# Sums of weight blocks of the second feed-forward, moved from on-chip adds to adding DMAs in memory that are issued during the first feed-forward

## The chip, the cores and the metric

The kernel runs on one core of a Trainium2 chip. The core has five engines with queues of their own: PE (TensorE, matrix products), DVE (VectorE), ACT (ScalarE), POOL (GpSimd) and SP (SyncE, which here only issues DMAs), and 16 DMA engines that move data between memory and the core's on-chip buffer. The metric is the device time in microseconds. Three timed runs of the kernel before lie between 1104.29 and 1104.48 us, median 1104.42.

## The reference

One transformer layer, all in float32, on 512 latent tokens and 256 context tokens of width 1024, in three steps. Each token stream first gets half a step of a gated feed-forward; then the latent tokens are mixed (attention over latent and context keys beside a gated chunk MLP); then the latent tokens alone get a second half step of feed-forward with other weights.

```python
def swiglu(h, w1, w3, w2):
    return (jax.nn.silu(h @ w1) * (h @ w3)) @ w2      # w1, w3: 1024 x 2816, w2: 2816 x 1024

def ffn_sublayer(h_in, shift, scale, gate, norm_w, w1, w3, w2):
    h = modulate(rms_norm(h_in, norm_w), shift, scale)
    return h_in + 0.5 * gate * swiglu(h, w1, w3, w2)

    x = ffn_sublayer(x, ...ffn1...)          # 512 latent tokens
    ctx = ffn_sublayer(ctx, ...ffn1...)      # 256 context tokens, same weights
    ...                                      # token mixing: x from x and ctx
    x = ffn_sublayer(x, ...ffn2...)          # 512 latent tokens, weights ffn2
    return x, ctx
```

## The kernel before

**Precision.** A float32 operand is split in two: `oph` is a copy rounded to the fp32r type (ACT, a CAST) and `opl` is the rest (DVE, a subtraction). `Stream.operand` and `split` (L141 and L142) do this for a weight operand. `mm3` (L176 to L178) makes each product from three matmuls: high by high, high by low, low by high.

**Units.** The hidden width 2816 of a feed-forward is worked off in 22 units `f` of 128 columns. The first four units of each feed-forward are plain products. For the other 18 (4 to 21) the class `Winograd` uses a fast 2 by 2 block product: the two weight matrices w1 and w3 of a unit are cut over the 1024 rows into four quarters of 128x512 elements that lie side by side in one weight block `wst[...]` of 128x2048 elements (1 MB), and seven products (B11, T1, B21, T2, T3, T4, B22) take the place of eight. Each product is 12 matmuls. A matmul has 384 columns in the first feed-forward (two halves of 768 tokens) and 256 in the second (two halves of 512).

The seven weight operands are quarters or sums of quarters. `prep` loads the block on SP's queue (`Stream.block`, L129) and `wants` hands out the operands in order. The sums are four 128x512 operations for each block, in place in the block's buffer: `s1 = q2 + q3`, `q2 = q0 - q2`, `q0 = s1 - q0` and, behind the split of the old `q1`, `q1 = q1 - q0`. They run on POOL in both feed-forwards, apart from block 4 of the second, whose four sums DVE does at the start of its units (`wino.prep(NPLAIN2, nc.vector)`); block 5 of the second is "held": its POOL sums wait for a small copy (`release`) so that they don't start early.

**Order.** A `Flow` is a queue of split operands ahead of PE: five pairs of buffers (`OPS`), up to four more in the second feed-forward (`MORE`). In both runs of units the order of every engine's instructions is that of the program (`nc.ordered`). Products take a pair, and the pair that is freed is filled with the next operand; so a split's lead over PE can't grow beyond the pairs.

**Between the units.** Runs of units are cut by down projections (the product with w2): in the first feed-forward behind units 6, 10 and 16 (`down_thirds`), where the weights come as 512 KB raw tiles (`raw<-wst`, L137). There, and at two slots of each unit, fillers (`ada_step`) work off the modulation vectors: a 512 KB tile of `w_ada` is loaded into one of three `raw` buffers (`raw<-wada`, L137), and DVE multiplies and reduces it. In the first feed-forward's first units POOL, DVE and SP work in these intervals: first down 135.8 to 181.0 us, units 7 to 10 from 181 to 235, second down to 280, units 11 to 16 to 363.4, third down 363.4 to 416.7, units 17 to 21 to about 480. Token mixing follows; the second feed-forward's seven-product units start at about 797 and the kernel's last matmul ends at 1099.45. `L60` in the profile is the helper that records all engine calls, so names of tiles tell more than lines there: `block` is a weight block or a sum in it, `s` is `s1`, `hh`/`hl` are the first feed-forward's inputs, `mm` and `one` are PSUM banks, `gh`/`gl` a unit's output.

```python
            def block_sums():
                if not self.ready[4]:
                    eng[0].tensor_sub(q[2], q[0], q[2])
                eng[0].tensor_sub(q[0], s1[0], q[0])
            def third():
                a = st.operand(q[1])
                eng[0].tensor_sub(q[1], q[1], q[0])
                return a
```

Of the kernel before, what the change touches and what calls it, by code (L numbers as in the profile page):

```python
# [17 lines left out]
P = 128  # L18
# [3 lines left out]
NF = FF // P  # L22
# [6 lines left out]
CHUNKS1 = [5, 5, 6, 6]  # L29
# [5 lines left out]
NPLAIN1 = 4  # L35
NPLAIN2 = 4
BLOCKS = 2
RAWS = 3
OPS = 5
MORE = 4  # L40
GA, GB = (0, 384), (384, 384)

COL_B, COL_N1, COL_N2, COL_N3 = 0, 72, 80, 88
# [138 lines left out]
def layer_kernel(ctx: ExitStack, tc: tile.TileContext, xT, wfirst, wst, wada, wuq, wkpe, cols, wrope, vnw, rope, out):  # L182
    nc = Core(tc)
    left = lambda: tc.using_default_side("left")
    right = lambda: tc.using_default_side("right")

    const = ctx.enter_context(tc.tile_pool(name="const", bufs=1))
    raws = ctx.enter_context(tc.tile_pool(name="raws", bufs=RAWS))
    opp = ctx.enter_context(tc.tile_pool(name="ops", bufs=1))
    st = Stream(nc, raws, opp, OPS, wst)  # L190
# [361 lines left out]
    r0, v = rstd_tiles(0)  # L552
# [286 lines left out]
    class Winograd:  # L839


        def __init__(self, pool, n, u0, blocks, g_tile, sl_bufs, s1_bufs, third=None, held=None):
            self.third, self.held = third, held
            self.sl_bufs, self.s1_bufs = sl_bufs, s1_bufs
            self.ready = (None,)
            self.pool, self.n, self.u0, self.blocks, self.g_tile = pool, n, u0, blocks, g_tile

        def tmp(self, name, n, bufs=1):
            return self.pool.tile([P, n], F32, tag=name, bufs=bufs, name=f"{name}_{nc.next_id()}")

        def prep(self, f, eng=None, early=False):
            r = st.block(wst, (self.u0 + 2 * f) // 2, self.third if f % 3 == 0 else None)
# [6 lines left out]
            self.ready = f, q, s1, nc.gpsimd if early else eng or nc.gpsimd, early  # L859

        def wants(self, f):
            q, s1, eng = [], [], []
# [28 lines left out]
            of = lambda i: lambda: st.operand(q[i])  # L891
            return first, lambda: st.operand(s1[0]), third, of(0), of(2), of(3), of(1)

        def plan(self, flow, f0, downs, late=False):

            self.flow, self.late = flow, f0 if late else -1
            w = self.wants(f0)
            flow.todo.append(w[0])
            for f in range(f0, NF):
                nxt = self.wants(f + 1) if f + 1 < NF else None  # L900
                nx = nxt[:1] if nxt else ()
                if f == self.late:
                    flow.todo.extend((w[3], w[4], w[2]) + nx + (w[1],) + w[5:])
                elif nxt is None:
                    flow.todo.extend((w[3], w[4], w[2], w[1]) + w[5:])
                else:
                    flow.todo.extend(w[1:5] + nx + w[5:])
# [30 lines left out]
        def unit(self, f, hd, step):  # L938
# [7 lines left out]
            def ev_sl():  # L946
                nc.scalar.activation(sl, X, AF.Silu)
                yield

            def ev_u2():  # L950
                v.tensor_add(u2, Y, p1)
                yield

            def ev_u2z():
                v.tensor_add(u2, Y, p1)
                yield
                v.tensor_add(Z, Z, u2)

            def ev_u3():
                nc.scalar.copy(u3, W)  # L960
                v.tensor_add(u3, Z, u3)
                yield

            def ev_lo():
                v.tensor_add(W, W, u2)
                v.tensor_mul(W, W, sl)
                yield
                g_split(W, gh[:, :n], gl[:, :n])
# [11 lines left out]
                yield  # L980

            def ev_u3b():
                v.tensor_add(u3, Z, u3)
                yield

            nxt = None
# [7 lines left out]
            else:  # L994
# [4 lines left out]
            seeded = f != self.late and f + 1 < NF  # L999
# [23 lines left out]
    def ada_step(n=1):  # L1023
        for _ in range(n):
            next(ada, None)
# [15 lines left out]
    t1ctx = ExitStack()  # L1041
    with right():
# [955 lines left out]
    i = LAST  # L1998
# [421 lines left out]
```

## Time and profile before

| what | value |
|---|---|
| median of three runs | 1104.42 us (1104.29 to 1104.48) |
| profiled execution | 1104.5 us |
| its span (first to last instruction) | 1102.5 us, so 2.0 us lie outside |
| TensorE clock granted | 1.00 |
| busiest engine | PE, 1097.5 us of the span |
| DVE, ACT, POOL busy | 892.8, 536.5, 310.3 us |
| DMA traffic on SP's queue | 124.63 MB, 33.2% of what 16 engines' span holds |

Busy times are of one core. A group's row has the count behind an x, then the busy time of all, the mean of one in ns, and behind the second bar the idle time just before such instructions with what ended it. A window's row has the stretch, its length, and for each engine the busy time and the count; then the granted clock, the share of time in which the 16 DMA engines were busy, and GB/s. A row of the timeline or the chain begins with the start and the length in microseconds. A bracket at a row's end is an idle time before it and its releaser.

### The profile page before, as it was taken

What the parts mean: (1) busy time and instruction counts of PE and PEld (TensorE: products, weight loads), DVE (VectorE), ACT (ScalarE), POOL (GpSimd) and SP (SyncE); (2) the same over time, 40 slices, a digit from 0 to 9 for tenths busy, and PEclk for the clock granted to TensorE, in tenths of its full rate; (3) what the DMA queues carried; (4) which work ended last, traced back from release to release, by engine and by line L of the source; (5) the groups of instructions that cost most, each with busy time, mean ns of one, the idle gap of its engine ahead of it and who ended that gap; (6) DMA issues with size and microseconds to landing.
All of it is one profiled execution on the core that took longest, in us unless ns stands there. A gap on an engine that the chain in (4) does not pass through costs nothing.

```text
span 1102.5 us, 19621 instructions
## 1 busy us (share of the span) xinstructions
PE 1097.5 (100%) x7610; PEld 1052.5 (95%) x7610; DVE 892.8 (81%) x1594; ACT 536.5 (49%) x1115; POOL 310.3 (28%) x269
## 2 busy tenths in 40 slices
PE   9999999999999999999999999999999999999998
PEld 7899999999999999999998889999999989898997
DVE  5779998888878769866867899989988878787883
ACT  6545422431344214443765549986663535354450
POOL 0003303311344013400009317860014444352420
PEclk9999999999999999999999999999999999999999
DMA  9721354234334664412241310103222322424202
GB/s 354 279 60 47 120 172 139 100 137 148 106 124 151 233 201 164 149 54 93 97 132 61 102 50 21 39 21 102 91 94 89 123 78 93 137 78 132 99 21 77
DMA packets 35677, 125.95 MB, mean 114 GB/s; under 512 B 3712, under 2 KB 10624, under 8 KB 30976
## 3 DMA queue, kind: packets, MB, share of 16 engines
q1 hardware_dynamic: 35440, 124.63, 33.2%
q8 instruction: 60, 0.98, 0.4%
q14 instruction: 33, 0.27, 0.1%
q10 hardware_dynamic: 144, 0.06, 0.1%
HBM read 122.58 MB, written 2.10 MB: 113 GB/s over the span
## 4 chain that ended last, share of the span: by engine, by line
PE 96%; DMA 1%; DVE 1%; ACT 1%; POOL 0%; issue 0%; SPq 0%; ACTq 0%; POOLq 0%; DVEq 0%
PE mm L60 61%; PE one L60 20%; PE big L60 10%; PE big L616 1%; PE mm L601 1%; DMA scale<-wada 1%; PE mm L177 1%; PE mm L176 1%; PE mm L178 1%; PE mm L338 1%; DMA x<-xT 0%; PE big L608 0%; DVE sq L60 0%; POOL pe L60 0%; ACT hh L60 0%
## 5 line engine op out<-in xcount | busy, mean ns | idle before, releaser
L60 DVE TENSOR_TENSOR opl<-block,oph 128x512 fp32r<-128x512 f32 x216 | 195.4, 912 | 32.6 <-ACT oph L60 29.9
L60 POOL TENSOR_TENSOR block<-block 128x512 f32<-128x512 f32 x69 | 105.0, 1522 | 378.9 <-DVE opl L60 376.2
L60 ACT CAST oph<-block 128x512 fp32r<-128x512 f32 x216 | 132.3, 622 | 108.8 <-PE mm L60 85.5
L60 PE MATMUL mm<-gl,oph 128*128 128x256 f32 (+2 forms) x573 | 176.4, 308 | 0.0
L60 PE MATMUL mm<-gh,opl 128*128 128x256 f32 (+2 forms) x573 | 176.4, 308 | 0.0
L60 PE MATMUL mm<-gh,oph 128*128 128x256 f32 (+2 forms) x573 | 176.4, 308 | 0.0
L60 PEld LDWEIGHTS mm<-gh,oph 128*128 128x128 f32 x573 | 107.6, 188 | 5.5
L60 PEld LDWEIGHTS mm<-gh,opl 128*128 128x128 f32 x573 | 107.6, 188 | 5.4
L60 PEld LDWEIGHTS mm<-gl,oph 128*128 128x128 f32 x573 | 107.6, 188 | 5.4
L60 ACT CAST oph<-raw 128x512 fp32r<-128x512 f32 x127 | 76.0, 620 | 69.7 <-PE mm L60 44.4
L60 DVE SCALAR_TENSOR_TENSOR x<-mm,g,x 128x512 f32<-128x512 f32 (+2 forms) x136 | 78.7, 600 | 28.5 <-PE mm L60 27.9
L60 DVE TENSOR_TENSOR opl<-raw,oph 128x512 fp32r<-128x512 f32 x127 | 88.1, 710 | 15.3 <-ACT oph L60 14.0
L60 POOL TENSOR_TENSOR block<-s,block 128x512 f32<-128x512 f32 x35 | 48.3, 1379 | 123.8 <-DVE opl L60 122.3
L60 PE MATMUL mm<-hh,oph 128*128 128x384 f32 (+2 forms) x195 | 64.9, 333 | 0.0
L60 PE MATMUL mm<-hl,oph 128*128 128x384 f32 (+2 forms) x195 | 64.8, 333 | 0.0
L60 PE MATMUL mm<-hh,opl 128*128 128x384 f32 (+2 forms) x195 | 64.8, 333 | 0.0
L60 DVE SCALAR_TENSOR_TENSOR junk<-raw,cb 128x1024 bf16<-128x1024 f32 x48 | 62.1, 1308 | 0.2 <-DMA raw<-wada 0.2
L60 POOL TENSOR_TENSOR s<-block 128x512 f32<-128x512 f32 x34 | 53.7, 1579 | 11.4 <-DMA block<-wst 11.4
L60 DVE SCALAR_TENSOR_TENSOR raw<-raw,cb 128x1024 f32<-128x1024 f32 x32 | 42.1, 1322 | 8.3 <-DMA raw<-wada 8.2
L60 PE MATMUL one<-hl,oph 128*128 128x384 f32 x144 | 48.1, 334 | 0.0
L60 PE MATMUL one<-hh,oph 128*128 128x384 f32 x144 | 48.1, 334 | 0.0
L60 PE MATMUL one<-hh,opl 128*128 128x384 f32 x144 | 48.1, 334 | 0.0
(699 smaller groups left out, 3361.9 us busy)
## 6 DMA issues: line engine op xcount, KB each, us to landing
raw<-wst SPq DMA_DIRECT2D x77, 512.0 KB, 3.8
block<-wst SPq DMA_DIRECT2D x36, 1024.0 KB, 4.9
raw<-wada SPq DMA_DIRECT2D x56, 512.0 KB, 4.3
scale<-wada SPq DMA_DIRECT2D x16, 512.0 KB, 9.0
x<-xT SPq DMA_DIRECT2D x5, 512.0 KB, 6.4
raw<-wfirst SPq DMA_DIRECT2D x8, 256.0 KB, 8.8
out<-x SPq DMA_DIRECT2D x7, 256.0 KB, 2.3
raw<-wuq SPq DMA_DIRECT2D x2, 384.0 KB, 5.1
```

The source lines that it names most:

```text
L60: return lambda *a, **k: self.tc.keep_in_program_order(f(*a, **k))
L176: nc.tensor.matmul(out, lh, rh, start=first, stop=False, skip_group_check=more)
L177: nc.tensor.matmul(out, lh, rl, start=False, stop=False, skip_group_check=more)
L178: nc.tensor.matmul(out, ll, rh, start=False, stop=last, skip_group_check=more)
L338: pin(nc.tensor.matmul(pa[q, :P], scw[:, kt, 2 - 2 * w : 34 - 2 * w], units[d][w][:, kt * P : kt * P + P], start=w == 0 and kt < 4, stop=w ...
L601: pin(nc.tensor.matmul(o, l[:, c], r, start=k == 0 and m == 0 and w == 0, stop=k == NK - 1 and m == 2, skip_group_check=True))
L616: pin(nc.tensor.matmul(two(pbs[i]), ops[k][lo][:, i * P : i * P + P], lat(r, k), start=False, stop=k == NK - 1 and m == 2, skip_group_chec ...
```

## The change

The 18 blocks of the second feed-forward no longer get their sums on chip. 18 tiles `sums4` to `sums21` of 128x2048 elements (1 MB each) in device memory take them, and POOL's queue issues 144 DMAs from memory to memory of 128x512 elements (256 KB, in rows of 2 KB) during the first feed-forward: for each block four that copy and four that add to what lies there (`accum_op=ALU.add`), in batches of six blocks, step by step. With only additions the four sums come out as q2, q2+q3 and the like with other signs than before, so some on-chip signs are turned: `hA2`, the additions to `u2`, `Z` and `u3` in the evictions, and `u3`'s copy becomes an activation with scale -1. The number of DVE and ACT instructions in the evictions is the same.

The DMAs' places: two behind each of three slots in units 5 to 20 (six a unit, `ada_up`), and two behind each of the eight `ada_step(2)` of a down projection (16 a down, `after1`): 96 and 48.

In the second feed-forward `prep_sums` loads, for each block, 512 KB and 256 KB of the raw block (three quarters) and 1 MB of sums, 1.75 MB where it was 1 MB, all on SP's queue; there are two buffers for the sums, and a third block buffer goes. With that 69 POOL instructions (17 blocks by four, and the copy of `release`) and the four DVE sums of block 4 are gone. PE's instructions are the same 7050 in the same order.

```diff
+    block_sums = [dram.tile([P, 2048], F32, name=f"sums{f}") for f in range(NPLAIN2, NF)]
+        def prep_sums(self, f):
+            a = st.raw_pool.tile([P, 2048], F32, tag="block", bufs=BLOCKS, name=f"block_{nc.next_id()}")
+            src = wst[self.u0 // 2 + f]
+            nc.sync.dma_start(a[:, 0:1024], src[:, 0:1024])
+            i = f - NPLAIN2
+            pool = st.more[0] if i % 2 else self.pool
+            t = pool.tile([P, 2048], F32, tag=f"sums{i % 2}", bufs=1, name=f"s_{nc.next_id()}")
+            nc.sync.dma_start(t, block_sums[i])
+            nc.sync.dma_start(a[:, 1536:2048], src[:, 1536:2048])
+            q = [t_[:, j * 512 : j * 512 + 512] for t_, j in ((a, 0), (t, 0), (a, 1), (t, 1), (t, 2), (a, 3), (t, 3))]
...
             def ev_u3():
-                nc.scalar.copy(u3, W)
-                v.tensor_add(u3, Z, u3)
+                if neg:
+                    nc.scalar.activation(u3, W, AF.Copy, scale=-1.0)
+                    v.tensor_sub(u3, u3, Z)
...
     def after1(flow, f):
         for ci in ends1(f):
-            down_thirds(flow, starts1[ci], CHUNKS1[ci], lambda dt: ada_step(2))
+            down_thirds(flow, starts1[ci], CHUNKS1[ci], lambda dt: (ada_step(2), next(summing, None), next(summing, None)))
+
+    def sum_steps():
+        q = lambda t, i: t[:, i * 512 : i * 512 + 512]
+        for b in range(0, NF - NPLAIN2, BATCH):
+            for dst, src, add in ((2, 0, 0), (0, -2, 0), (2, -2, 1), (0, -3, 1), (1, 2, 0), (1, -3, 1), (3, 1, 0), (3, -1, 1)):
+                for i in range(b, b + BATCH):
+                    t = block_sums[i]
+                    a = q(wst[U_UP2 // 2 + NPLAIN2 + i], -src) if src < 0 or (dst, add) == (2, 0) else q(t, src)
+                    nc.gpsimd.dma_start(q(t, dst), a, accum_op=ALU.add if add else ALU.bypass)
+                    yield
+
+    summing = sum_steps()
...
     def ada_up(f, i):
...
+        if f > NPLAIN1:
+            next(summing, None)
+            next(summing, None)
...
-            nc.vector.tensor_sub(hA2, hA2, hB2)
+            nc.vector.tensor_sub(hA2, hB2, hA2)
...
-    wino = Winograd(f2, 256, U_UP2, blocks, g2_tile, 2, 2, f2, NPLAIN2 + 1)
-    wino.prep(NPLAIN2, nc.vector)
+    wino = Winograd(f2, 256, U_UP2, blocks, g2_tile, 2, 2, True)
+    wino.prep_sums(NPLAIN2)
```

What this does to the order of instructions is seen at three places.

First, POOL's queue in a unit of the first feed-forward (unit 8 into unit 9, about 205 to 222 us in the profile before). `s1` and `block` are the on-chip sums of the first feed-forward's own blocks, which stay; before, they stand in a row:

```order
L60 TENSOR_TENSOR block_2340_2341<-block_2340_2341 128x512
L60 TENSOR_TENSOR s1_2517_2518<-block_2514_2515 128x512
L60 TENSOR_TENSOR block_2514_2515<-block_2514_2515 128x512
L60 TENSOR_TENSOR block_2514_2515<-s1_2517_2518,block_2514_2515 128x512
L60 TENSOR_TENSOR block_2514_2515<-block_2514_2515 128x512
```

and now:

```order
L61 TENSOR_TENSOR block_2389_2390<-block_2389_2390 128x512
L61 DMA sums6_63<-wst 128x512
L61 DMA sums7_64<-wst 128x512
L61 TENSOR_TENSOR s1_2572_2573<-block_2569_2570 128x512
L61 TENSOR_TENSOR block_2569_2570<-block_2569_2570 128x512
L61 TENSOR_TENSOR block_2569_2570<-s1_2572_2573,block_2569_2570 128x512
L61 DMA sums8_65<-wst 128x512
L61 DMA sums9_66<-wst 128x512
L61 DMA sums4_61<-sums4_61 128x512
L61 DMA sums5_62<-sums5_62 128x512
L61 TENSOR_TENSOR block_2569_2570<-block_2569_2570 128x512
```

Two issues now stand ahead of `s1`, and four between the third sum of a block and its last one (`q1`).

Second, POOL's queue at the third down projection (behind unit 16, 363.4 to 416.7 us). Before, the fourth sum of unit 17's block follows the third at once in the queue:

```order
L60 TENSOR_TENSOR block_4322_4323<-block_4322_4323 128x512
L60 TENSOR_TENSOR s1_4502_4503<-block_4499_4500 128x512
L60 TENSOR_TENSOR block_4499_4500<-block_4499_4500 128x512
L60 TENSOR_TENSOR block_4499_4500<-s1_4502_4503,block_4499_4500 128x512
L60 TENSOR_TENSOR block_4499_4500<-block_4499_4500 128x512
```

Now 18 issues stand between those two, of which these are the last ten, with the sum behind them:

```order
L61 DMA sums20_77<-wst 128x512
L61 DMA sums21_78<-wst 128x512
L61 DMA sums16_73<-wst 128x512
L61 DMA sums17_74<-wst 128x512
L61 DMA sums18_75<-wst 128x512
L61 DMA sums19_76<-wst 128x512
L61 DMA sums20_77<-wst 128x512
L61 DMA sums21_78<-wst 128x512
L61 DMA sums16_73<-wst 128x512
L61 DMA sums17_74<-wst 128x512
L61 TENSOR_TENSOR block_4618_4619<-block_4618_4619 128x512
```

The 18 go over one step of the list to the next: ten copies and eight adds. The first down projection has 18 issues between the same two sums as well (six copies, twelve adds), the second 16 (twelve and four).

Third, the start of the second feed-forward's units on DVE, at about 797 us. `ds` is a small difference ahead of it, `sl` a product of a plain unit behind it; before:

```order
L60 TENSOR_TENSOR ds<-s_87 128x4
L60 TENSOR_TENSOR s_10347_10348<-block_10345 128x512
L60 TENSOR_TENSOR opl_10353<-block_10345,oph_10351 128x512
L60 TENSOR_TENSOR block_10345<-block_10345 128x512
L60 TENSOR_TENSOR block_10345<-s_10347_10348,block_10345 128x512
L60 TENSOR_TENSOR sl_10359<-big_9759,sl_10359 128x256
```

and now:

```order
L61 TENSOR_TENSOR ds<-s_108 128x4
L61 TENSOR_TENSOR opl_10519<-block_10510,oph_10517 128x512
L61 TENSOR_TENSOR sl_10523<-big_9924,sl_10523 128x256
L61 SCALAR_TENSOR_TENSOR t3l<-hfB,ds,t3h 128x256
L61 TENSOR_TENSOR t4l<-hfA,t4h 128x256
```

Three of block 4's sums are gone here, and the fourth a few rows below. On SP's queue each block's one load becomes three; before:

```order
L137 DMA raw_11485_11486<-wst 128x1024
L129 DMA block_11114_11115<-wst 128x2048
L129 DMA block_11297_11298<-wst 128x2048
L129 DMA block_11619_11620<-wst 128x2048
L129 DMA block_11791_11792<-wst 128x2048
```

and now (`s` is the tile of sums):

```order
L138 DMA raw_11638_11639<-wst 128x1024
L858 DMA block_11090_11091<-wst 128x1024
L863 DMA block_11090_11091<-wst 128x512
L862 DMA s_11093_11094<-sums7_64 128x2048
L858 DMA block_11270_11271<-wst 128x1024
L863 DMA block_11270_11271<-wst 128x512
L862 DMA s_11273_11274<-sums8_65 128x2048
```

The loads of block 4 and its sums stand ahead of these, in the place of the loads of before.

More of the change, by code (lines that the diff above doesn't have):

```diff
@@ L839, in layer_kernel, with __init__ @@
     class Winograd:
-        def __init__(self, pool, n, u0, blocks, g_tile, sl_bufs, s1_bufs, third=None, held=None):
-            self.third, self.held = third, held
+        def __init__(self, pool, n, u0, blocks, g_tile, sl_bufs, s1_bufs, summed=False):
+            self.third, self.held, self.summed, self.q = None, None, summed, {}
             self.sl_bufs, self.s1_bufs = sl_bufs, s1_bufs
@@ L849, in tmp, with wants_sums, first @@
             return self.pool.tile([P, n], F32, tag=name, bufs=bufs, name=f"{name}_{nc.next_id()}")
+        def prep_sums(self, f):
[8 more added lines that the diff above has]
+            q = [t_[:, j * 512 : j * 512 + 512] for t_, j in ((a, 0), (t, 0), (a, 1), (t, 1), (t, 2), (a, 3), (t, 3))]
+            self.ready = f, q
+        def wants_sums(self, f):
+            def first():
+                if self.ready[0] != f:
+                    self.prep_sums(f)
+                self.q[f] = self.ready[1]
+                return st.operand(self.q[f][0])
+            return [first] + [(lambda i=i: st.operand(self.q[f][i])) for i in range(1, 7)]
         def prep(self, f, eng=None, early=False):
@@ L948, in ev_sl, with add_u2, seed @@
                 yield
+            neg = self.summed
+            def add_u2():
+                if neg:
+                    v.tensor_sub(u2, p1, Y)
+                else:
+                    v.tensor_add(u2, Y, p1)
+            def seed():
+                if neg:
+                    v.tensor_sub(Z, u2, Z)
+                else:
+                    v.tensor_add(Z, Z, u2)
             def ev_u2():
-                v.tensor_add(u2, Y, p1)
+                add_u2()
                 yield
             def ev_u2z():
-                v.tensor_add(u2, Y, p1)
+                add_u2()
                 yield
-                v.tensor_add(Z, Z, u2)
+                seed()
             def ev_u3():
-                nc.scalar.copy(u3, W)
-                v.tensor_add(u3, Z, u3)
+                if neg:
+                    nc.scalar.activation(u3, W, AF.Copy, scale=-1.0)
+                    v.tensor_sub(u3, u3, Z)
+                else:
+                    nc.scalar.copy(u3, W)
+                    v.tensor_add(u3, Z, u3)
                 yield
             def ev_lo():
-                v.tensor_add(W, W, u2)
+                if neg:
+                    v.scalar_tensor_tensor(W, W, -1.0, u2, ALU.mult, ALU.subtract)
+                else:
+                    v.tensor_add(W, W, u2)
                 v.tensor_mul(W, W, sl)
@@ L982, in ev_u3b @@
             def ev_u3b():
-                v.tensor_add(u3, Z, u3)
+                if neg:
+                    v.tensor_sub(u3, Z, u3)
+                    seed()
+                else:
+                    v.tensor_add(u3, Z, u3)
                 yield
@@ L998, in unit @@
                 self.product(banks[3], "T3", True, ev_u3())
-            seeded = f != self.late and f + 1 < NF
+            seeded = neg or f != self.late and f + 1 < NF
             if f + 1 < NF and nxt is None:
```

14 lines of the change are left out of this document (10 added, 4 removed).

## The prediction, made before the changed kernel ran

> **What bounds the kernel now.** I read the page first: engines, chain by engine, the DMA queue, and the groups that the change touches.
>
> ```profile
> span 1102.5 us, 19621 instructions
> PE 1097.5 (100%) x7610; PEld 1052.5 (95%) x7610; DVE 892.8 (81%) x1594; ACT 536.5 (49%) x1115; POOL 310.3 (28%) x269
> q1 hardware_dynamic: 35440, 124.63, 33.2%
> PE 96%; DMA 1%; DVE 1%; ACT 1%; POOL 0%; issue 0%; SPq 0%; ACTq 0%; POOLq 0%; DVEq 0%
> L60 DVE TENSOR_TENSOR opl<-block,oph 128x512 fp32r<-128x512 f32 x216 | 195.4, 912 | 32.6 <-ACT oph L60 29.9
> L60 DVE TENSOR_TENSOR opl<-raw,oph 128x512 fp32r<-128x512 f32 x127 | 88.1, 710 | 15.3 <-ACT oph L60 14.0
> L60 POOL TENSOR_TENSOR block<-block 128x512 f32<-128x512 f32 x69 | 105.0, 1522 | 378.9 <-DVE opl L60 376.2
> ```
>
> PE is busy in 1097.5 of 1102.5 us, and 96% of the chain that ended last is PE. POOL, which the change relieves, holds 0% of the chain. Then I read the windows and, in the chain in order of time, the steps of the second feed-forward.
>
> ```profile
> core 0: us, PE busy (x) PEld busy (x) DVE busy (x) ACT busy (x) POOL busy (x), PEclk, DMA share, GB/s
> 135.00:490.00 355.00, 355.00 (x2454) 355.00 (x2453) 292.32 (x492) 123.14 (x232) 86.07 (x57) 1.00 0.44 149
> 135.80:181.00 45.20, 45.20 (x389) 45.20 (x389) 41.81 (x78) 9.21 (x17) 6.02 (x3) 1.00 0.50 160
> 235.00:280.00 45.00, 45.00 (x388) 45.00 (x387) 38.85 (x65) 9.18 (x16) 6.02 (x3) 1.00 0.44 151
> 363.40:416.70 53.30, 53.30 (x460) 53.30 (x460) 38.45 (x62) 10.28 (x19) 6.02 (x3) 1.00 0.62 213
> 876.00:936.00 60.00, 60.00 (x438) 56.36 (x437) 49.39 (x75) 27.90 (x61) 23.58 (x16) 1.00 0.30 102
> 218.39 2.08 PE mm L60 x12
> 796.91 17.68 PE mm L60 x156
> 814.59 1.36 PE one L60 x12
> 1099.32 0.13 PE mm L178
> ```
>
> The chain from 796.91 to 1099.45 (1099.32 + 0.13) is PE behind PE, and in every window PE's busy time is the window's length. A product of 12 matmuls lasts 2.08 us in the first feed-forward and 1.36 in the second, so a unit of seven takes 14.56 and 9.52 us. So work taken from POOL and DVE can't shorten the second feed-forward while PE is fed; the question is whether the first, which gets 144 DMAs, stays as full.
>
> **Part 1: the second feed-forward, value 0.** 68 POOL sums of 1.4 to 1.6 us go, none of them on the chain. Four DVE sums go from its start:
>
> ```profile
> 797.93 0.69 DVE L60 TENSOR_TENSOR s<-block 128x512 f32<-128x512 f32 x1
> 798.53 0.69 DVE L60 TENSOR_TENSOR opl<-block,oph 128x512 fp32r<-128x512 f32 x1
> 799.13 0.68 DVE L60 TENSOR_TENSOR block<-block 128x512 f32<-128x512 f32 x1
> 799.85 0.69 DVE L60 TENSOR_TENSOR block<-s,block 128x512 f32<-128x512 f32 x1
> 806.68 0.69 DVE L60 TENSOR_TENSOR block<-block 128x512 f32<-128x512 f32 x1
> 993.67 0.69 DVE L60 TENSOR_TENSOR opl<-block,oph 128x512 fp32r<-128x512 f32 x1
> 997.10 0.28 PE L60 MATMUL mm<-b22h,opl 128*128 128x256 f32 x1
> block<-wst SPq DMA_DIRECT2D x36, 1024.0 KB, 4.9
> ```
>
> Together 2.75 us; PE is inside one step of 17.68 us at that time, so they are cover and not chain: 0. The turned signs keep the count of instructions, so 0 as well. The loads grow from 1 to 1.75 MB a unit. The queue's row gives the engines' rate: 124.63 MB in 0.332 x 1102.5 = 366 us is 340 GB/s, so 1.75 MB (1.84e6 bytes) is 5.4 us of a 9.52 us unit. A whole block landed 4.9 us after its issue, and each operand needs its own piece only. The smallest lead that I found of a split over PE is 997.10 - 994.36 = 2.7 us. POOL's sums (four in a row, 6 us) no longer stand between load and split, which is more than the 2.3 us (5.4 less 3.1 for 1 MB) by which the load grows. I take 0; the bound upward would be one late load at the start, 5.4 - 2.7 = 2.7 us.
>
> **Part 2: POOL issues 144 DMAs.** No row shows POOL issuing such a DMA. From below, SP issues one in 0.33 us; from above, POOL's own operation of the same 128x512 size took 1.52. I take 1.5, for it is the same engine that would have to prepare 128 rows. The first feed-forward's own sums stand behind them in POOL's queue:
>
> ```profile
> 201.46 0.33 SPq L129 DMA_DIRECT2D block<-wst  x1
> 202.97 0.68 DVE L60 TENSOR_TENSOR opl<-s,oph 128x512 fp32r<-128x512 f32 x1
> 210.26 0.33 PE L60 MATMUL one<-hh,opl 128*128 128x384 f32 x1
> 205.74 1.29 POOL L60 TENSOR_TENSOR block<-block 128x512 f32<-128x512 f32 x1 [7.17 <-DVE opl L60]
> 207.79 1.32 POOL L60 TENSOR_TENSOR s<-block 128x512 f32<-128x512 f32 x1 [0.77 <-DMA block<-wst]
> 209.19 1.74 POOL L60 TENSOR_TENSOR block<-block 128x512 f32<-128x512 f32 x1
> 211.63 1.30 POOL L60 TENSOR_TENSOR block<-s,block 128x512 f32<-128x512 f32 x1 [0.69 <-DVE opl L60]
> 220.30 1.29 POOL L60 TENSOR_TENSOR block<-block 128x512 f32<-128x512 f32 x1 [7.37 <-DVE opl L60]
> 410.02 2.14 POOL L60 TENSOR_TENSOR block<-block 128x512 f32<-128x512 f32 x1 [53.87 <-DVE opl L60]
> ```
>
> POOL's work per unit is 1.29 + 1.32 + 1.74 + 1.30 = 5.65 us, in 14.56. Six issues add 9.0: 14.65, just full. Four of them fall in the idle 7.37 us ahead of the last sum (6.0), two ahead of `s`, which starts 3.0 us behind 207.03 instead of at 207.79, so 2.2 late. The split of `s` ends at 203.65 and PE reads it at 210.26, a lead of 6.6 us, which covers this. Value 0, and POOL becomes the bound above (14.56 - 5.65)/6 = 1.49 us an issue once the lead is used up. In the third down projection 18 issues (27 us) lie in an idle 53.87 us.
>
> The gap between 912 ns for `opl<-block` and 710 ns for `opl<-raw` (195.4 us in 216) shows DVE and POOL in each other's way: 0.2 x 216 = 44 us. The Trainium skill, "SBUF — State Buffer", section "SBUF: two separate sides", lets the two engines share a port pair under an exclusive lock, taken by a DVE operation with two on-chip inputs only against a POOL operation that reads the on-chip buffer; by that a DMA issue, which reads none, would cost these splits nothing, while the gap that the sums cause would vanish from the second feed-forward. No run here shows yet what an issue does to the splits.
>
> **Part 3: the DMA engines.** 256 KB at 340 GB/s is 0.77 us of all 16 engines; no row shows a transfer from memory to memory. A copy that reads and writes at once costs 0.77, one that pays for both 1.54; an add reads two and writes one, so 1.54 to 2.31. I take the lower ends, for reading and writing are one pass in the loads of the row too. 72 x 0.77 + 72 x 1.54 = 166 us (277 by the upper ends) go into the 355 us of the second row, where loads take 0.44 x 355 = 156 us: 322 of 355, it fits. By the upper ends it is 433.
>
> In places it is tighter. The third down projection has the fullest engines, 0.62 x 53.3 = 33 us, and ten copies and eight adds are 20.0: 53.0 of 53.3. The first has 22.6 + 23.1 = 45.7 of 45.2 us, but DVE's waits there (the first row, from the waits of 135 to 185 us) are small; in the third (the second row, 363 to 425 us) they are not:
>
> ```profile
> DVE junk L60 <- DMA raw<-wada: 0.2, 1, 0.2
> DVE raw L60 <- DMA raw<-wada: 8.2, 6, 2.3
> 419.74 1.88 DVE L60 TENSOR_TENSOR opl<-block,oph 128x512 fp32r<-128x512 f32 x3
> 423.15 0.33 PE L60 MATMUL one<-u3h,opl 128*128 128x384 f32 x1
> ```
>
> Six waits make 8.2 us. DVE's other idle time in that stage is 53.3 - 38.45 - 8.2 = 6.65 us. The splits behind them lead PE by 2.7 us (the first of the three ends at about 420.4). If one of the new transfers stands ahead of each awaited load, DVE loses 6 x 0.77 to 6 x 1.54 = 4.6 to 9.2 us, which 6.65 + 2.7 = 9.35 holds. I take 0. The sums themselves are needed only at 797 and their last issue stands in unit 20, before 475 us (416.7 + 4 x 14.56), so they can't be late.
>
> **The sum:** 0 + 0 + 0 against the profiled 1104.5 us (its span of 1102.5 and 2.0 outside), which lies 0.1 above the median; I put 1104.6, for a small loss is nearer than a gain.
>
> **Rivals.**
> A, the third down's loads come late. It is slower by one mechanism: transfers of POOL's queue stand ahead of the `raw<-wada` loads, and DVE, which does these in order, hands its next splits over late. With two ahead of each (mean 1.11 us over ten copies and eight adds) 13.3 us are lost, 13.3 - 9.35 = +4.0; with two adds 18.5, +9.1; by the upper ends (mean 1.88) 22.6, +13.2. It decides from 9.35 us on: 1108.5 to 1117.7. For it speaks the 0.62, against it the three raw buffers. The Trainium skill, "DMA: Bandwidth & Descriptors", section "Issuing engines are not separate DMA queues", says that DMAs issued by GpSimd and Sync end up on the same 16 engines and interleave there; that would be this rival's mechanism, and no run here shows it yet.
> B, POOL becomes the bound. If an issue must also wait for the end of a DVE split (0.68 us), it takes 1.5 + 0.68 = 2.2 us, and a unit asks for 5.65 + 13.2 = 18.85, 4.3 over. Units with issues come in runs of 4, 6 and 4 between the downs: 17.2 + 25.8 + 17.2 less the lead of 6.6 each time is +40: 1145; at 2.0 us (3.1 over) it is +23.6: 1128. For it: issues have no row here, and 1.49 is close to the 1.5 taken. Against it: POOL's own arithmetic at 1.5 reads and writes 256 KB, an issue none. The Trainium skill's page on SBUF warns in the same section that a DVE operation in a two-port mode keeps GpSimd from writing its DMA descriptors until it ends, which would be such a wait. The Trainium skill, "DMA: Bandwidth & Descriptors", section "Latency and other measured facts", has about 1 us to the first byte for a DMA of GpSimd; by that estimate POOL would be at 5.65 + 6 = 11.65 of 14.56, and nothing of B would be left.
> C, the DMA engines are the bound: 433 us of work in 355 by the upper ends is +78, less little: 1180. Against it, both ends would have to be the worst.
> D, faster: PE waits at the second feed-forward's start for DVE in some way the chain hides; at most the 2.75 us of the four sums: 1101.8. Against it, PE's step there has no gap.
>
> **How the numbers follow.** No change 0.57, A 0.24, B 0.10, C 0.06, D 0.03. Within 0.2% (2.2 us, about what a measurement of this kernel can tell) lies the first; A, B and C are slower, 0.40; D is faster. No change and A hold 0.81, so the range is from 1103.4 (a little of D's gain) to 1118 (A by the upper ends). No change alone would be 1103.4 to 1106.6.
>
> **What would show it.** Right: PE's busy time equal to the window's in all of 135 to 490 us; the waits for `raw<-wada` in 363 to 425 at 8 to 17 us and no PE idle behind them; POOL's issues near 1.5 us; DMA share near 0.9 in the downs; in the second feed-forward `opl` splits near 700 ns and PE unchanged. Wrong: PE idle behind `opl` at 420 (A), POOL without idle time in units 7 to 16 and splits waiting for `s` (B), DMA share at 1.0 with all loads late (C), or a second feed-forward shorter than 302 us (D).

## The result, and the profile after

The changed kernel takes 1348.93 us (median of four runs, 1346.68 to 1353.66), the kernel before 1104.36 in the same session: a ratio of 1.222, 95% interval 1.2183 to 1.2258. The prediction was no change, with a range up to 1118 us. The page of the changed kernel (new beside the lines shown of before: `q0`, the queue of POOL's DMAs, and POOL's issues as a group):

```profile
span 1348.8 us, 19756 instructions
PE 1129.8 (84%) x7610; PEld 1078.7 (80%) x7610; DVE 854.4 (63%) x1590; ACT 536.7 (40%) x1115; POOL 302.3 (22%) x344
q1 hardware_dynamic: 40624, 138.79, 30.5%
q0 software_dynamic: 16128, 37.76, 18.7%
PE 52%; issue 32%; POOL 13%; DMA 2%; DVE 1%; ACT 1%; POOLq 0%; SPq 0%; DVEq 0%; ACTq 0%
L61 POOL DMA_DIRECT2D sums<-wst x108 | 79.2, 737 | 406.2 <-issue 398.4 <-DVE x L61 7.5
sums<-wst POOLq DMA_DIRECT2D x108, 256.0 KB, 6.4
```

PE's share of the chain falls from 96 to 52%, and 32% is "issue", time in which an engine waits for nothing that the profile shows. The group's row says whose: POOL stood idle for 406.2 us ahead of its issues from `wst`, all but 8 of it "issue", and its own time for an issue is short (737 ns). Of the 246.3 us that the span grew (1348.8 - 1102.5), 214.0 are idle time of PE (219.0 against 5.0) and 32.3 longer busy time, at a lower granted clock. The waits (total us, times, longest), then windows: two stretches of the first feed-forward and the second one's units:

```profile
POOL sums L61 <- issue: 419.7, 94, 9.7
ACT oph L61 <- POOL block L61: 159.5, 22, 25.3
ACT oph L61 <- POOL s L61: 109.1, 10, 21.6
PE one L61 <- ACT u L61: 132.6, 7, 42.8
181.00:235.00 54.00, 29.11 (x159) 28.47 (x157) 19.99 (x33) 9.69 (x18) 16.52 (x19) 0.78 0.57 115
350.00:400.00 50.00, 7.60 (x35) 7.61 (x36) 9.11 (x15) 5.23 (x10) 13.66 (x14) 0.59 0.47 85
1042.50:1345.00 302.50, 302.39 (x2162) 282.57 (x2161) 206.10 (x382) 135.08 (x290) 0.00 (x0) 1.00 0.42 141
```

The cause reads down the first four rows: POOL waits ahead of an issue, the sums `block` and `s` behind it in POOL's queue come late, so do ACT's splits of them, and what stands behind these in ACT's queue, and PE. In 350 to 400 us PE works in 7.60 of 50. No engine is full there, and the DMA engines are at 0.47. The second feed-forward is as full as before: 302.39 of 302.50. One such wait in order of time, ACT's queue and then PE's:

```profile
391.35 0.62 ACT L61 CAST oph<-s 128x512 fp32r<-128x512 f32 x1 [21.57 <-POOL s L61]
391.87 0.47 ACT L61 COPY u<-one 128x384 f32<-128x384 f32 x1
392.40 0.69 PE L61 MATMUL one<-u4h,oph 128*128 128x384 f32 x1 [42.78 <-ACT u L61]
392.88 0.52 PE L61 MATMUL one<-u4l,oph 128*128 128x384 f32 x1
393.20 0.52 PE L61 MATMUL one<-u4h,opl 128*128 128x384 f32 x1
```

ACT waited 21.57 us for the sum `s` and did the eviction `u` behind it only then; PE, idle for 42.78 us, waited for that eviction. Its first matmuls after the idle time follow each other by 0.32 us and not 0.173 (2.08 us for 12, before): the granted clock was 0.50 from 392.4 to 395.8 us, and 0.59 over the stretch of 350 to 400. That is where the longer busy time comes from.

POOL's queue in order of time, at the first down projection, shows the wait itself. The first group's issues are copies, from 144.49 on they add:

```profile
129.76 1.56 POOL L61 DMA_DIRECT2D sums<-wst  x3
135.98 1.70 POOL L61 DMA_DIRECT2D sums<-wst  x3 [4.67 <-issue]
144.49 0.89 POOL L61 DMA_DIRECT2D sums<-wst  x1 [6.81 <-issue]
149.35 0.85 POOL L61 DMA_DIRECT2D sums<-wst  x1 [3.97 <-issue]
157.28 0.82 POOL L61 DMA_DIRECT2D sums<-wst  x1 [7.07 <-issue]
```

Three copies go out in 1.6 us, and then POOL stops. The trace has the landing of each transfer: 62 of the 144 issues began 0.28 to 0.34 us after the landing of the very one before (all 62 are adds behind adds, one add under way at a time; those at 149.35 and 157.28 are such), and 105 that long after the landing of one of the last four. Of the copies, three were under way at most. An add landed 6.39 us after its issue on average, a copy 5.37, and from the first issue to the last landing it takes 630 us, from 116 to 746.

To see where time goes, the start of the same matmul, counted from the program's first, is compared in both traces (each has 7610 matmuls in the same order; the 7050 given with the change is not what the traces have); the table gives by how many us it is later than before, at places that are named by the time before.

| kernel | 135.8 | 181 | 235 | 280 | 363 | 416.7 | 450 | 500 | 797 | 1095 |
|---|---|---|---|---|---|---|---|---|---|---|
| changed | -0.1 | 1.8 | 56.3 | 59.0 | 147.2 | 175.0 | 203.1 | 245.6 | 245.5 | 245.5 |
| e1_no_sums | 0.0 | 0.0 | -0.1 | -0.1 | -0.1 | -0.1 | -0.1 | -0.1 | -0.1 | -0.1 |
| e2_ring768 | 0.0 | 7.2 | 15.2 | 20.1 | 30.5 | 47.9 | 47.9 | 58.8 | 58.5 | 58.4 |
| e10_ring1280 | 0.5 | 8.5 | 14.4 | 26.8 | 41.8 | 56.3 | 60.9 | 70.0 | 69.6 | 69.6 |
| e4_copies | 0.2 | 1.6 | 2.9 | 7.7 | 11.7 | 22.6 | 24.6 | 28.0 | 27.7 | 27.7 |
| e14_copies1280 | 0.0 | 8.3 | 8.3 | 17.7 | 22.5 | 33.3 | 35.4 | 40.2 | 39.9 | 39.8 |
| e13_sp_pinned | 0.2 | 0.2 | 0.1 | 0.1 | 0.1 | 0.1 | 6.9 | 7.0 | 6.6 | 6.6 |
| e11_tiny512 | -0.1 | -0.2 | 0.4 | 0.4 | 13.0 | 15.0 | 29.2 | 32.4 | 32.1 | 32.0 |
| e12_tiny1280 | -0.1 | -0.1 | -0.2 | -0.2 | -0.2 | -0.2 | 0.7 | 0.8 | 0.6 | 0.5 |

In the changed kernel the whole loss is made between 135.8 and 490 us by the times of before, in the units and downs that hold the issues; ahead of them and behind them nothing is lost.

### The profile page after: what moved, and what is told of

Same layout as the page of the kernel before. It is cut to its first block, busy times and chain, and to the rows that moved or that the text cites. A ratio compares the mean times of both kernels' runs of the same rounds, so it can differ in the third digit from the quotient of the medians.

```text
span 1348.8 us, 19756 instructions
## 1 busy us (share of the span) xinstructions
PE 1129.8 (84%) x7610; PEld 1078.7 (80%) x7610; DVE 854.4 (63%) x1590; ACT 536.7 (40%) x1115; POOL 302.3 (22%) x344
## 3 DMA queue, kind: packets, MB, share of 16 engines
q1 hardware_dynamic: 40624, 138.79, 30.5%
q0 software_dynamic: 16128, 37.76, 18.7%
## 4 chain that ended last, share of the span: by engine, by line
PE 52%; issue 32%; POOL 13%; DMA 2%; DVE 1%; ACT 1%; POOLq 0%; SPq 0%; DVEq 0%; ACTq 0%
PE mm L61 32%; PE big L61 8%; PE one L61 7%; POOL sums L61 7%; POOL block L61 5%; POOL s L61 1%; PE big L620 1%; PE mm L605 1%; DMA scale<-wada 1%; PE mm L179 1%; PE mm L178 1%; PE mm L177 1%; DMA block<-wst 1%; PE mm L342 0%; DMA x<-xT 0%
## 5 line engine op out<-in xcount | busy, mean ns | idle before, releaser
L61 DVE TENSOR_TENSOR opl<-block,oph 128x512 fp32r<-128x512 f32 x162 | 119.7, 747 | 168.7 <-ACT oph L61 166.9
L61 ACT CAST oph<-block 128x512 fp32r<-128x512 f32 x162 | 99.8, 620 | 263.3 <-POOL block L61 159.5
L61 PE MATMUL mm<-gh,oph 128*128 128x256 f32 (+2 forms) x573 | 179.2, 313 | 8.2 <-DVE x L61 7.6
L61 POOL DMA_DIRECT2D sums<-wst x108 | 79.2, 737 | 406.2 <-issue 398.4
L61 PE MATMUL one<-u4h,oph 128*128 128x384 f32 x36 | 18.2, 506 | 142.8 <-ACT u L61 132.6
L61 DVE TENSOR_TENSOR opl<-s,oph 128x512 fp32r<-128x512 f32 x90 | 67.8, 758 | 107.1 <-ACT oph L61 105.4
L61 PEld LDWEIGHTS one<-u4h,oph 128*128 128x128 f32 x36 | 10.3, 286 | 145.3 <-ACT u L61 134.9
L61 ACT CAST oph<-s 128x512 fp32r<-128x512 f32 x90 | 55.7, 620 | 151.4 <-POOL s L61 109.1
L61 PE MATMUL mm<-u4h,oph 128*128 128x384 f32 x36 | 15.8, 439 | 61.2 <-ACT u L61 61.2
L61 PEld LDWEIGHTS mm<-u4h,oph 128*128 128x128 f32 x36 | 8.9, 246 | 62.8 <-ACT u L61 62.8
```

The source lines that it names most:

```text
L61: return lambda *a, **k: self.tc.keep_in_program_order(f(*a, **k))
```

## The experiments

The theories have letters of their own, which are not those of the prediction's rivals. R: the room in which POOL's DMAs keep their descriptors, the notes that tell the DMA engines what to move (`dynamic_dma_scratch_size`, 512 in the changed kernel), holds three copies or one add, and a further issue waits until one lands. S: adds to memory go one at a time whatever the room. E: the DMA engines need this long for such transfers, whatever the room. D, which came up with e3: the transfers fill the DMA engines and hold up the first feed-forward's loads. The times of e2, e4, e8, e10 and e11 are single runs; each loss below is told from that session's own time before (1104.1 to 1104.3).

**e1_no_sums**, the second feed-forward alone:

```diff
-            nc.sync.dma_start(t, block_sums[i])
+            nc.sync.dma_start(t, src)
...
-                    nc.gpsimd.dma_start(q(t, dst), a, accum_op=ALU.add if add else ALU.bypass)
+                    pass
```

> The 144 adding and copying DMAs are left out; the second feed-forward loads its sums' tile from the raw block, so its values aren't the reference's, but it moves the same bytes. All theories that put the loss into the first feed-forward's DMAs expect the time of before, 1102.2 to 1106.6 us, and a second feed-forward of 302.5 us from its first seven-product unit to the last matmul. If the larger loads (1.75 MB a unit) or the turned signs cost something, it shows here alone: 1107 to 1115.

1104.26 us, a ratio of 1.0001 (0.9991 to 1.001). The second feed-forward with 1.75 MB of loads a unit, without 69 POOL and four DVE instructions, and with turned signs costs nothing and gains nothing. Part 1 of the prediction holds.

**e2_ring768** and **e3_ring1600**, more room:

```diff
-    const.tile([P, 64], F32, name="pad_scratch")
-    nc = bacc.Bacc(..., dynamic_dma_scratch_size=512)
+    nc = bacc.Bacc(..., dynamic_dma_scratch_size=768)
```

The tile `pad_scratch` of 256 bytes goes. e3 has 1600, and three buffers for `s1` in place of four make the room; so it is in e8, e10, e12 and e14.

> Only the space for POOL's DMA descriptors changes, 768 bytes of a partition for 512 (the pad of 256 gives it). Theory R (the space is full: at 512 bytes three copies or one add are under way, and the next issue waits for a landing): five copies and two adds should be under way, an add's interval falls from about 6.9 us to 3 to 3.5, a unit with six adds asks POOL for about 24 us in place of 47, and the time falls to 1150 to 1200 us. Theory S (adds to memory go one at a time whatever the space): adds stay at one, 1320 to 1350. Theory E (the DMA engines themselves need this long for transfers from memory to memory): 1340 to 1360.

> The space for descriptors is 1600 bytes; it comes from the pad and from one of four buffers for s1. R: eleven copies or five adds fit, POOL's wait for space is nearly gone, a unit asks for 5.65 + 6 x 0.8 = 10.5 of 14.56 us, and the time is 1104 to 1125 us. S: adds still one at a time, 1300 to 1350. E: 1330 to 1360.

e2 took 1163.9 us: 256 bytes of room took back 185 of the 244.6 us lost. In its trace five copies were under way at most and two adds, and from one add to the next issue it was 3.99 us (6.20 in the changed kernel). S and E fall. e3 took 1185.25 us (ratio 1.0705 to 1.0765), slower than e2 though POOL's waits for room were nearly gone:

```profile
POOL sums L61 <- issue: 192.3, 74, 9.3
POOL sums L61 <- issue: 25.5, 17, 5.5
PE 69%; DMA 17%; DVE 9%; issue 2%; ACT 2%; POOL 0%; ACTq 0%; SPq 0%; DVEq 0%; POOLq 0%
ACT oph L61 <- DMA block<-wst: 57.0, 13, 9.4
POOL s L61 <- DMA block<-wst: 53.0, 12, 8.2
```

The first row is e2's, the other four are e3's. With more room the waits for "issue" fall from 192.3 to 25.5 us, and waits for the loads of weight blocks, 110.0 us, stand in their place. R expected 1104 to 1125 of e3, and missed: there is a second cost behind the first. Part of e3's loss (about 9 us) also came in the second feed-forward; see e10.

**e4_copies**, every DMA a copy (no sums are formed):

```diff
-                    nc.gpsimd.dma_start(q(t, dst), a, accum_op=ALU.add if add else ALU.bypass)
+                    nc.gpsimd.dma_start(q(t, dst), a)
```

> All 144 are plain copies, none adds, so the sums' values aren't the reference's; space of 512 bytes. R: three under way at all times, about 1.9 us an issue, a unit asks for 5.65 + 11.4 = 17, some 2.5 over: 1110 to 1140 us. S: no adds, so no serial ones: 1104 to 1120 if copies can go freely, but then more than three must be seen under way. E with engines that need 5 us for each transfer: above 1300.

1133.2 us, within what R gave, with three under way at most and 133.8 us of waits. It prices the transfers too. `q0` had 12.2% of 16 engines over 1131.0 us here, and 18.2% over 1161.7 us in e2, for the same bytes:

```profile
q0 software_dynamic: 11520, 37.76, 12.2%
q0 software_dynamic: 16128, 37.76, 18.2%
```

So a copy of 256 KB takes 0.96 us of all engines (138 us over 144), and an add 1.97 ((211 - 69) us over 72). The time of packets isn't a fixed price, though: the same 144 DMAs took 195 us in e3 (16.5% of 1182.0) and 252 in the changed kernel (18.7% of 1348.8).

**e5_contig**, the same sums in fewer rows (a second copy of the blocks with each quarter in one piece):

```diff
-        q = lambda t, i: t[:, i * 512 : i * 512 + 512]
+        q = lambda t, i: t[32 * i : 32 * i + 32, :]
...
+    wq = np.ascontiguousarray(wst[44 + NPLAIN2 : 44 + NF].reshape(18, P, 4, 512).transpose(0, 2, 1, 3)).reshape(18, P, 2048)
```

> The same 144 sums with the space of 512 bytes, but from a copy of the weights in which each quarter lies in one piece, so that a DMA of 256 KB is 32 rows of 8 KB in place of 128 of 2 KB. R (space is counted in rows): about ten copies and six adds fit, the waits of one add at a time are gone. What then is left is a second theory, D, on why 1600 bytes gave 1185 and not 1104: the DMA engines' time. If an add's 1.97 us of all engines (18.2% of 16 engines over 1161.7 us, less 72 copies at 0.96) goes with bytes, D stays: 1150 to 1190 us. If it goes with rows, the engines are freed as well: 1104 to 1125. S (adds always one at a time): above 1300.

1154.31 us (ratio 1.0437 to 1.0468). With a room of 512 bytes as in the changed kernel but a quarter of the rows, up to eight copies or six adds were under way and POOL's waits for "issue" were 17.2 us. In e11 below, with all the rows and a thirty-second of the bytes, it was three copies or one add again. So the room is counted in rows, not in the bytes that are moved. Loads stay late (DMA 14% of the chain, weight blocks landed after 9.2 us), as D has it, and 49 us are lost by 500 us, with four buffers for `s1`.

```profile
q0 software_dynamic: 6912, 37.76, 13.4%
```

The same bytes took 154 us of the engines here (13.4% of 1151.7) and 211 in e2, so an add's 1.97 us holds for rows of 2 KB only.

**e6_half** and **e7_half768**, one DMA at each place, 76 in all (blocks from the seventh on get no sums), with 512 and 768 bytes:

```diff
-            next(summing, None)
-            next(summing, None)
+            next(summing, None)
...
-... lambda dt: (ada_step(2), next(summing, None), next(summing, None)))
+... lambda dt: (ada_step(2), next(summing, None)))
```

> One DMA at each place in place of two, 76 in all; blocks from the seventh on load raw weights for their sums, so values aren't the reference's. Space of 512 bytes. R: three adds of 5 to 6.9 us, one behind the other, are 15 to 21 us of a unit's 14.56, but copies come between and POOL waits only where the space is full: 1106 to 1130 us, far less than half of the change's loss. If the loss went with the number of DMAs, half of it would stay: about 1230.

> As e6_half with 768 bytes of space, so two adds fit. R: POOL hardly waits. D: 40 copies at 0.96 and 36 adds at 1.97 are 109 us of the engines beside 156 for loads in 355: 0.75 of the engines. 1104 to 1112 us; more if the engines hold up single loads already at that share.

1146.67 (1.0368 to 1.0399) and 1141.55 us (1.0312 to 1.0391). Half the DMAs lose 42 us, a sixth of 245, so the loss isn't in proportion. Both were more than expected (up to 1130 and 1112): D was undervalued, for the engines were busy in only 0.67 of the time from 135 to 490 us in e7, and its block loads still landed after 9.9 us, where e1's took 6.0.

**e8_small**, e3's 1600 bytes with a quarter of the bytes moved (no sums formed):

> As e3_ring1600, but each of the 144 DMAs moves only 128 of the 512 columns (64 KB in 128 rows of 512 bytes); the second feed-forward loads raw weights for its sums, so values aren't the reference's. Rows and issues are the same, bytes a quarter. D by bytes: the engines are freed, loads come in time, 1104 to 1115 us. D by rows: 1150 to 1190 as before.

1120.85 us, of which about 9 again came in the second feed-forward; at 500 us the loss was 6.8. Rows and issues are those of e3, which stood at 69.6 there: most of D goes with bytes.

**e9_sp_copies**, copies issued by SP:

```diff
-                    nc.gpsimd.dma_start(q(t, dst), a, accum_op=ALU.add if add else ALU.bypass)
+                    nc.sync.dma_start(q(t, dst), a)
```

> All 144 are plain copies and SP issues them at 0.33 us each, at the same places of the program, so POOL issues none and waits for no space; values of the sums aren't the reference's. With POOL issuing, the same copies gave 1133.2 us. D (transfers in the engines hold up the first feed-forward's loads): most of that stays, 1112 to 1135 us. R alone (POOL's waits for space hold up its sums): nothing stays, 1104 to 1107.

1173.39 us (1.0605 to 1.064), but not at the change's places: the copies ran from 15 to 200 us, since SP's queue isn't held to the program's order. All of the 70 us were lost by 181 us, none later. It doesn't tell the theories apart; e13 does it again.

**e10_ring1280**, e3 with 1280 bytes:

> As e3_ring1600 with 1280 bytes of space, four adds. Everything on chip then lies 512 bytes from where it lay with 768, and not 832 as with 1600. With 1600 the matmuls of 256 columns went from 113.7 to 118.7 ns in the second feed-forward (9.4 us lost there). If the address does that, they are at 113.7 again and the second feed-forward at 302.5 us: 1158 to 1176 in all, a loss of the first feed-forward between that of 768 bytes (58.6) and of 1600 (69.4). If the missing fourth buffer of s1 did it: 1168 to 1190.

1174.94 us. The first feed-forward's loss is 70.0, as with 1600, though POOL waits longer for "issue" (45.8 us against 25.5), and the second's is gone. So R's limit is out of the way here, and what is left, 49 us in e5 to 70, is D's. Whether the missing fourth buffer of `s1` has a part in the 70 was not tried by itself; without late loads it costs next to nothing (e12).

**e11_tiny512** and **e12_tiny1280**, the 144 DMAs with 64 bytes a row (no sums formed), with 512 and 1280 bytes of room:

```diff
-        q = lambda t, i: t[:, i * 512 : i * 512 + 512]
+        q = lambda t, i: t[:, i * 512 : i * 512 + 16]
```

> The change's 144 DMAs with the space of 512 bytes, each of 128 rows but only 16 of 512 columns (64 bytes a row); the second feed-forward loads raw weights for its sums, so values aren't the reference's. Bytes are gone, rows are not. R: an add still waits for the landing of the one before, now 2.5 to 4 us: six of them and 5.65 us are 21 to 30 us of a unit's 14.56 in every second unit: 1140 to 1220 us. D: 1104 to 1110.

> As e11_tiny512 with 1280 bytes of space: neither waits for space nor bytes are left, only POOL's issues (0.55 us a copy, 0.85 an add, so at most 5.65 + 5.1 = 10.75 of 14.56 us). R and D: 1103 to 1107 us. If issues between POOL's sums cost by themselves: 1110 to 1130.

1137.05 us and 1106.05 us (ratio 1.0006 to 1.0025). POOL's waits, e11 first:

```profile
POOL sums L61 <- issue: 176.0, 74, 7.1
POOL sums L61 <- issue: 9.6, 9, 2.1
```

So waiting for room costs 33 us by itself where an add lands in 3.5 us (R gave 1140 to 1220 us, just above), and 144 issues by themselves cost 1 to 3 us.

**e13_sp_pinned**, **e14_copies1280** and **e15_pin_only**, what D is:

```diff
-        self.pinned = {e: Pinned(tc, getattr(tc.nc, e)) for e in ("vector", "scalar", "gpsimd", "tensor")}
+        self.pinned = {e: Pinned(tc, getattr(tc.nc, e)) for e in ("vector", "scalar", "gpsimd", "tensor", "sync")}
```

This stands in e13 (e9's copies) and e15 (e1's kernel without any); e14 is e10 with copies only.

> 144 plain copies issued by SP, with SP's queue held to the program's order in the two feed-forwards, so that they stand at the change's places; values of the sums aren't the reference's. If loads held up in the engines are enough (D alone), about what POOL's copies lost with a space of 512 bytes (28 us) stays on top of e15_pin_only. If the lead of 6.6 us covers late loads as long as POOL isn't late as well, 0 to 8 us on top of e15_pin_only.

> 144 plain copies issued by POOL with 1280 bytes of space (eight under way), so POOL hardly waits for space; values aren't the reference's. With 512 bytes these copies lost 28 us with 134 us of POOL's waits. If the waits for space made these: 1104 to 1112 us. If late loads made them: 1125 to 1145, more under way being no help.

> No sums at all (as e1_no_sums), but SP's queue held to the program's order in both feed-forwards: the control for e13_sp_pinned. 1104 to 1112 us; what it loses is the price of that order alone.

1111.09 (1.0049 to 1.0079), 1144.29 (1.0345 to 1.0393) and 1104.13 us (0.9989 to 1.0009). The order alone costs nothing. The same 37.76 MB of copies lose 7 us when SP issues them in its own queue, and 40 when POOL does with room enough. Both lose by late loads:

```profile
403.57 7.87 DMA raw<-wada
415.42 9.00 DMA block<-wst
137.09 11.56 DMA raw<-wada
block<-wst SPq DMA_DIRECT2D x18, 1024.0 KB, 4.8
block<-wst SPq DMA_DIRECT2D x18, 1024.0 KB, 4.9
block<-wst SPq DMA_DIRECT2D x18, 1024.0 KB, 9.5
block<-wst SPq DMA_DIRECT2D x18, 1024.0 KB, 6.0
```

The first two rows are from e13's chain around the end of the third down projection; the only place where it loses is just behind, at the start of unit 17. The third is from e14's chain at the start of the first down projection, by the end of which it has lost 8 us. The last four are the landing of the first feed-forward's whole weight blocks: 4.8 us in e13 and 4.9 in e15, its control without the copies; 9.5 in e14 and 6.0 in e1, where no sums are issued and SP's queue is free, as in e14. With POOL's transfers a block comes 3.5 us later, with SP's no later. The `w_ada` loads came late in both (6.0 us in e13 against 5.2 in e15, 5.5 in e14 against 4.4 in e1), and e13 lost 7 us in all. Why transfers of POOL's queue hold up a block's load and the same transfers of SP's queue don't was not settled. In e14 POOL's issues also stand ahead of the sums, the room is larger and `s1` has a buffer less, and no run had the late loads by themselves.

## Why the prediction was wrong, and where it was right

Part 1 was right, with its cover: the second feed-forward keeps its 302.5 us (e1, and the changed kernel itself). Its splits did become faster, and it changed nothing:

```profile
L60 DVE TENSOR_TENSOR opl<-block,oph 128x512 fp32r<-128x512 f32 x108 | 107.5, 1004 | 11.7 <-ACT oph L60 9.6
L61 DVE TENSOR_TENSOR opl<-block,oph 128x512 fp32r<-128x512 f32 x54 | 36.8, 687 | 8.4 <-ACT oph L61 7.6
```

The rows are the groups of before and of after within the second feed-forward. What the Trainium skill's page "SBUF — State Buffer" (section "SBUF: two separate sides") says, that a DVE operation with two on-chip inputs, as such a split is, is held up only against a POOL operation that reads the on-chip buffer, agrees with the changed kernel's trace. Up to 760 us the splits of `block` and `s` that ran beside one of POOL's issues and no sum took 688 ns on average (22 of them, none over 694), those beside neither 686 (67), and those beside a sum of POOL over 1100 (37).

Part 2 is the step that failed. It priced an issue as work of POOL, between SP's 0.33 and POOL's 1.52 us, and took 1.5. The work was less: 0.53 us a copy and 0.83 an add. But an issue also waited until an earlier transfer had landed, a wait that the prediction put at nothing: 6.20 us went by from one add to the next issue. Six of them are 37.2 us in a unit of 14.56. A row near to that stood in the prediction, 4.9 us to the landing of a block: 6 x 4.9 = 29.4 us would have given a loss in every unit of adds. Rival B named the right bound, POOL, and the right place, the sums that stand behind the issues, and a part of its sign came: ACT's splits waited 109.1 us for `s`. Its mechanism was another, a wait for the end of a DVE operation: an add's issue took 0.83 us whether DVE worked beside it (34 of them) or not (38). Its price of 2.0 to 2.2 us an issue was too low for the adds by a factor of three. The sentence on the Trainium skill's 1 us to the first byte ("DMA: Bandwidth & Descriptors", section "Latency and other measured facts"), by which nothing of B was left, went wrong in the same way: it is about when bytes start, and POOL was held by when they had all landed. The same page of the Trainium skill also says, in section "SWDGE vs HWDGE vs iDMA", that descriptors of DMAs issued from GpSimd go into rings in a part of the on-chip buffer; that POOL waits when that room is full was the step missing, and e2, e5 and e11 against e12 show it. The change had a line on it, which the diff ahead of the prediction doesn't show: `dynamic_dma_scratch_size` went from 256 to 512, beside a pad of 256 bytes. The prediction gave it no price.

Part 3 was right within its bounds on the engines' time (0.96 us a copy and 1.97 an add in e4 and e2; 195 to 252 us in all, between the 166 and 277 given) and rival A's mechanism is real. In e13 the loss came where A put it, behind the third down projection, and its 6.9 us lie in A's 4.0 to 13.2, though these were copies of SP's queue and a late weight block had its part. With POOL's own transfers it is larger, 40 to 70 us, and comes in all three downs and some units: a `w_ada` load landed after 11.56 us, where the prediction let one or two transfers of 0.77 to 1.54 us stand ahead of it. That term was mis-sized, with up to eight transfers under way. The first down projection, which the prediction passed over with 45.7 us of transfers for 45.2 because DVE waited only 0.2 us there, lost 8 us in e14. And the splits' lead over PE (2.7 and 6.6 us) was set against late sums in part 2 and against late loads in part 3, each by itself, though both lie on one chain: load, sums, split, product. That their delays add up there is argued; no run shows it by itself.

Together: the issues alone 1 to 3 us (e12), waiting for room at short landings 33 (e11), transfers with more room 70 (e10), and both at once 245, more than their sum. The waits fit this: each lasts as long as a landing, and an add landed after 3.5 us in e11 and 6.39 in the changed kernel.

No version tried is faster than before, and e1 shows why: even with the sums for nothing, the time is that of before.

## What to carry to other kernels

An issue of a DMA can hold its queue for as long as earlier transfers take to land: price it by the landing rows too, count how many fit the room for descriptors by their rows (an add took that of two to three copies, at 768 and 512 bytes), and look at what stands behind it in the same queue. A cover may be spent once: where delays lie on one chain, add them up before they are held against the lead. And where PE is full, as in this second feed-forward, work taken from other engines is worth nothing, and moving it elsewhere can only lose.

## What the runs showed of the hardware that was not expected

The size of POOL's room changed the speed of matmuls that ran long after its last transfer. With 1600 bytes, 832 more than the 768 of the changed kernel's room and pad, the second feed-forward's matmuls of 256 columns followed each other by 118.7 ns and not 113.7; with 1280 bytes, 512 more, by 113.7 again. e3 and e10 differ in nothing else, and e8 has the 118.7 with a quarter of the bytes moved. The room shifts where the tiles behind it lie on chip, and that is the likely cause; no run moved the tiles by themselves. In windows of 302 us, e3 first, then e10:

```profile
876.00:1178.00 302.00, 302.00 (x2088) 282.21 (x2087) 200.56 (x365) 130.50 (x278) 0.00 (x0) 1.00 0.43 141
866.60:1168.60 302.00, 302.00 (x2161) 282.42 (x2160) 206.13 (x381) 134.94 (x290) 0.00 (x0) 1.00 0.43 141
```

PE is "busy" all the time in both, at clock 1.00, but does 2088 matmuls in the one and 2161 in the other, the number of before. And an add of two tensors in memory took twice a copy's time in the DMA engines with rows of 2 KB (1.97 against 0.96 us for 256 KB, by e2 and e4), and less than that with rows of 8 KB: all 144 together took 154 us in e5 and 211 in e2.
